# Latent attention: score chunks of 1024 keys in place of 512, and a rule by width for who turns the probabilities

## The chip, the cores and the metric

The kernel runs on one core of one Trainium2 chip. The metric is the device time of one execution in microseconds. Three runs of the kernel before gave 3594.26, 3597.3 and 3606.11 us: the median is 3597.3 us.

## The reference

A trunk of two layers over 2048 tokens of width 1024. Layer 0 mixes tokens with sliding-window attention, layer 1 with multi-head latent attention, and each is followed by a mixture of 32 experts. The change lies in the attention of layer 1 alone. There, for each of 16 heads, with 96 numbers in a query or a key and 64 in a value:

```python
sc = einsum('bqhd,bkhd->bhqk', q, k) * scale
sc = where(kpos <= qpos, sc, -inf)
p = softmax(sc)
o = einsum('bhqk,bkhd->bqhd', p, v)
```

## The kernel before

**Units.** The function `attend` (L1326) works through 256 units. A unit is one head `h` and one block `i` of 128 queries; it sees `i + 1` blocks of 128 keys, so a head has 136 blocks of 128 x 128 probabilities and the whole stage 2176. Within a head the order is 15, 0, 14, 1, ... 8, 7 (the last head runs 0 to 15), so that a large unit and a small one make a pair of 17 blocks, 8 pairs in a head.

**Scores (`scores`, L1380).** A unit's keys are cut into chunks of 512, so a unit has one to four of them, a head 40 and the stage 640. Each chunk takes one PSUM bank from `room()` (L1343), which hands out the seven buffers `sc`. TensorE multiplies high and low halves of queries and keys in three products (L1393 to L1395) and adds the causal mask to the last block (L1397). VectorE takes the maximum of the chunk (L1398); with more than one chunk a second small reduction joins the maxima (L1403). Only then does ScalarE compute the exponentials into a float32 buffer `bpr` (L1407, seven buffers), which frees the bank.

**Turning.** The product with the values needs the probabilities transposed, as a high and a low float16 half. `direct` (L1370) gives about a fifth of the keys to TensorE, by a running debt (`owed[2]`), and in the last head all of the units from 13 on. The others go by a transfer: the high half is copied by VectorE (L1422, two fifths) or ScalarE (L1424), GpSimd subtracts it to make the low half (L1425; VectorE does a sixteenth), the two go into a pack `bpp` of up to 8 blocks (`place`, L1346), and `send` (L1356) has SyncE turn the pack into `bpt` with one transposing transfer (L180). Chunks of different units can share a pack. `turn_unit` (L1429) does TensorE's part two units later: up to four transposes into one bank of `room()` (L1437), ScalarE's copy of the high half (L1441), VectorE's subtraction for the low half (L1442).

**Values (`values`, L1444).** Six units later (`LAG`) TensorE multiplies the turned blocks with the values (L1456, L1457), two instructions a block, and VectorE sums the result of a pair out of PSUM (L1463).

**Order.** In each step of the loop over units the chunks of the new unit's scores alternate with those of the values of the unit six back, then come the turns of the unit two back, and in every second step one entry of `todo`: keys or values of a later head pair (which also take a bank from `room()`), the end of a pair (`finish`, L1471), or output weights. The order in which each engine's queue is written is fixed at build time by a scheduler that follows this program order but moves work that it takes to be ready ahead of work that it takes to be waiting. All transfers of the stage are issued by SyncE, in one queue. The eight PSUM banks are seven `sc` and one `po`.

Of the kernel before, what the change touches and what calls it, by code (L numbers as in the profile page):

```python
# [9 lines left out]
F32 = mybir.dt.float32  # L10
# [110 lines left out]
class Kernel:  # L121
# [1204 lines left out]
    def attend(self, q_d, kr_d, o_d, w_o):  # L1326
        nc, tc = self.nc, self.tc
        V, G, C = nc.vector, nc.gpsimd, nc.scalar
        LAG, PACK, SHARES, TURNED = 6, 8, (2 / 5, 1 / 16), 1 / 5
        with ExitStack() as s:  # L1330
            kp = s.enter_context(tc.tile_pool(name="tb", bufs=1, reuse_waits="tile"))
            wk = s.enter_context(tc.tile_pool(name="tk", bufs=2, reuse_waits="tile"))
# [3 lines left out]
            qb = [self.t(kp, [96, 2, S], F16, f"qb{n}") for n in range(2)]  # L1336
            for n in range(3):
                nc.sync.dma_start(kb[n][NOPE:], kr_d)
            U, heads, todo, owed = {}, {}, [], [0.0, -150.0, 0.0]

            pack = {"n": 0}

            def room():  # L1343
                return self.t(ps, [P, 512], F32, "sc", bufs=7)

            def place(nb):  # L1346
                if pack["n"] + nb > PACK:
# [21 lines left out]

            def direct(h, i, w):  # L1370

                owed[2] += TURNED * w
                if h == B_H - 1 and i >= 13:
                    return True
                if owed[2] > w / 2:
                    owed[2] -= w
                    return True
                return False

            def scores(n, h, i, u, c):  # L1380

                (Qh, Ql), (Kh, Kl) = ([b[h % len(b)][:, x] for x in range(2)] for b in (qb, kb))
                qs = slice(i * P, (i + 1) * P)
                nk = (i + 1) * P
                ncn = -(-nk // 512)
                if c == 0:
                    u["sm"], u["sc"], u["pt"], u["pr"] = self.t(wk, [P, 8], F32, "bsm2", bufs=4), [], [], []
                sm = u["sm"]
                w = min(512, nk - 512 * c)
                ks = slice(512 * c, 512 * c + w)  # L1390
                sc = room()
                last = c == ncn - 1
                nc.tensor.matmul(sc[:, :w], Qh[:, qs], Kh[:, ks], start=True, stop=False)  # L1393
                nc.tensor.matmul(sc[:, :w], Qh[:, qs], Kl[:, ks], start=False, stop=False)  # L1394
                nc.tensor.matmul(sc[:, :w], Ql[:, qs], Kh[:, ks], start=False, stop=not last)  # L1395
                if last:
                    nc.tensor.matmul(sc[:, w - P:w], self.ident_b, self.causal, start=False, stop=True)  # L1397
                V.tensor_reduce(sm[:, c:c + 1], sc[:, :w], axis=AX.X, op=ALU.max, negate=ncn == 1)  # L1398
                u["sc"].append((sc, w))
                if not last:  # L1400
                    return
                if ncn > 1:
                    V.tensor_reduce(sm[:, 4:5], sm[:, 0:ncn], axis=AX.X, op=ALU.max, negate=True)  # L1403
                nm = sm[:, 4:5] if ncn > 1 else sm[:, 0:1]
                for sc, w in u["sc"]:
                    pr = self.t(wk, [P, 512], F32, "bpr", bufs=7)
                    C.activation(pr[:, :w], sc[:, :w], AF.Exp, bias=nm)  # L1407
                    if direct(h, i, w):
                        u["pr"].append((len(u["pt"]), pr, w))
                        u["pt"].append(None)  # L1410
                        continue
                    pp, pt = place(w // P)
                    u["pt"].append(pt)
                    pb = pr[:, :w].rearrange("p (k q) -> p k q", q=P)

                    mine = [False, False]
                    for part, share in enumerate(SHARES):
                        owed[part] += share * w
                        if owed[part] > w / 2 and not (part and mine[0]):
                            mine[part], owed[part] = True, owed[part] - w  # L1420
                    if mine[0]:
                        V.tensor_copy(pp[:, :, 0], pb)  # L1422
                    else:
                        C.activation(pp[:, :, 0], pb, AF.Copy)  # L1424
                    (V if mine[1] else G).tensor_tensor(pp[:, :, 1], pb, pp[:, :, 0], op=ALU.subtract)  # L1425
                if n % 2 and (h == B_H - 1 or n == len(units) - 1):
                    send()

            def turn_unit(u):  # L1429

                many = len(u["pr"]) > 1
                for c, pr, w in u["pr"]:
                    if many and c % 2 == 0:
                        two = self.t(wk, [P, PACK, 2, P], F16, "bpt", bufs=9)
                    tp = room()
                    for k in range(0, w, P):
                        nc.tensor.transpose(tp[:, k:k + P], pr[:, k:k + P], self.ident)  # L1437
                    out = two[:, c % 2 * 4:] if many else self.t(wk, [P, 4, 2, P], F16, "bpd", bufs=5)
                    out = u["pt"][c] = out[:, :w // P]
                    tp = tp[:, :w].rearrange("p (k q) -> p k q", q=P)  # L1440
                    C.activation(out[:, :, 0], tp, AF.Copy)  # L1441
                    V.tensor_tensor(out[:, :, 1], tp, out[:, :, 0], op=ALU.subtract)  # L1442

            def values(h, i, n, u, c):  # L1444

                second = n % 2
                j = units[n ^ 1][1]
                if c == 0 and not second:
                    U["po"] = self.t(ps, [P, 512], F32, "po", bufs=1)
                slot = i > j  # L1450
                po = U["po"][:, slot * 130:(slot + 1) * 130]
                v = self.vbs[h // 2 % 2]
                pt = u["pt"][c]
                for k in range(4 * c, min(4 * c + 4, i + 1)):
                    vv = v[:, k, h % 2]
                    nc.tensor.matmul(po, pt[:, k % 4, 0], vv, start=k == 0, stop=False)  # L1456
                    nc.tensor.matmul(po[:, :HD + 1], pt[:, k % 4, 1], vv[:, :HD + 1], start=False, stop=k == i)  # L1457
                if second and 4 * c + 4 > i:
# [47 lines left out]
            for n in range(len(units) + LAG):  # L1506
                ns = nv = 0
                if n < len(units):
                    h, i = units[n]
                    at = n % NT  # L1510
                    U[n] = {}
                    ns = i // 4 + 1
                    if at == LAG - 2 and h % 2 == 0:
                        deliver(h + 1)
                        if h + 2 < B_H:
                            todo += [lambda q=q, f=nxt[2]: f(q) for q in range(4)]
                        else:
                            todo += [lambda c=c: project_weights(c) for c in range(KC)]
                    if at == 0 and h % 2 and h + 2 < B_H:

                        out = [(kb[(h + 1 + e) % 3], slice(64 * e, 64 * e + 64)) for e in range(2)]
                        todo += [lambda q=q, f=nxt[1], o=out: f(q, o) for q in range(4)]
                    if at == 10 and h % 2 and h + 1 < B_H:
                        deliver(h + 1)
                        if h + 3 < B_H:
                            nxt = self.pair((h + 3) // 2, room)
                            nxt[0]()
                if n >= LAG:
                    hv, iv = units[n - LAG]
                    nv = iv // 4 + 1  # L1530
                for c in range(max(ns, nv)):
                    if c < ns:
                        scores(n, h, i, U[n], c)
                    if c < nv:
                        values(hv, iv, n - LAG, U[n - LAG], c)
                if n - 2 in U and U[n - 2]["pr"]:
                    turn_unit(U[n - 2])
                if n >= LAG:
                    del U[n - LAG]
                if todo and (n % 2 or n >= len(units) - NT):  # L1540
                    todo.pop(0)()
# [113 lines left out]
```

## Time and profile before

| | |
|---|---|
| profiled execution, its own time | 3594.12 us |
| its span, first to last instruction | 3592.2 us |
| mean granted TensorE clock | 0.927 |
| busy over the span: TensorE (PE), VectorE (DVE), ScalarE (ACT), GpSimd (POOL) | 83%, 77%, 59%, 44% |
| latent attention | from about 1704 to 2563 us of the span |

Busy times are unions of an engine's instructions; idle time is put down to the engine or transfer whose signal ended it. Matmuls overlap in the pipeline, so the duration of one in a row is longer than the distance to the next. A transfer's row gives the time in which SyncE's queue issued it; its landing comes later.

### The profile page before, as it was taken

To read this page: it belongs to the slowest core of one execution; us is meant where nothing else is said; L and a number is where in the kernel's file an instruction comes from. 1 tells how busy PE (TensorE), PEld (TensorE's weight loads), DVE (VectorE), ACT (ScalarE), POOL (GpSimd) and SP (SyncE) were. 2 spreads that over 40 slices of the span, in tenths; PEclk is the share of its full clock that TensorE was granted. 3 is DMA by queue.
4 is the path that set the end of the run, shared out by engine and by line. 5 is a ranking of instruction groups with operands and counts; after the bars stand their busy time and mean duration, and the time that the engine had idled before them with its cause. 6 is when DMAs were issued, how large, how long until landed. Compare 5 with 4: busy or idle time off the path is not lost. (4 is left out here: it accounts for less than half of the span.)

```text
span 3592.2 us, 83083 instructions
## 1 busy us (share of the span) xinstructions
PE 2973.6 (83%) x32611; PEld 2239.1 (62%) x32611; DVE 2767.1 (77%) x5272; ACT 2109.6 (59%) x3669; POOL 1576.8 (44%) x1562
## 2 busy tenths in 40 slices
PE   7888878699998886788888889887897799989960
PEld 3444443399988885344566556665443799988860
DVE  5776758788877787776788888788688788877858
ACT  5766622166667675543777777776411566677753
POOL 2544434412323325564566666666244123233245
PEclk9999989899999998899999999999998899999985
DMA  8988779899999998996799999999699899999996
GB/s 225 192 190 174 137 201 311 261 325 350 337 351 359 357 361 290 242 236 179 133 185 179 169 164 182 159 186 190 155 294 281 287 342 351 362 357 362 359 343 242
DMA packets 1112188, 930.56 MB, mean 259 GB/s; under 512 B 933633, under 2 KB 992257, under 8 KB 1060865
## 3 DMA queue, kind: packets, MB, share of 16 engines
q1 hardware_dynamic: 1078112, 817.04, 85.3%
q0 software_dynamic: 33664, 108.03, 8.2%
q8 instruction: 259, 4.24, 0.5%
q14 instruction: 153, 1.25, 0.1%
HBM read 538.32 MB, written 158.60 MB: 194 GB/s over the span
## 5 line engine op out<-in xcount | busy, mean ns | idle before, releaser
L176 DVE SCALAR_TENSOR_TENSOR wl<-raw,wh 128x2048 f16<-128x2048 f32 x322 | 843.2, 2625 | 186.4 <-ACT wh L171 185.6
L908 PE MATMUL pg<-xt,wh 128*128 128x128 f16 (+5 forms) x4096 | 819.9, 230 | 62.4 <-DMA xt<-xs 48.0
L910 PE MATMUL pg<-xt,wl 128*128 128x128 f16 (+5 forms) x4096 | 807.0, 230 | 43.1 <-DVE wl L176 42.9
L909 PE MATMUL pg<-xt,wh 128*128 128x128 f16 (+5 forms) x4096 | 819.2, 230 | 0.0
L171 ACT ACTIVATE wh<-raw 128x2048 f16<-128x2048 f32 x384 | 722.1, 1900 | 92.1 <-DMA raw<-in_moe_w_dram 85.3
L1425 POOL TENSOR_TENSOR bpp<-bpr,bpp 128x512 f16<-128x512 f32 (+3 forms) x448 | 475.8, 1080 | 277.9 <-DVE bpp L1422 179.3
L938 POOL DMA_DIRECT2D y<-yr x256 | 146.3, 573 | 717.9 <-DVE yr L930 541.8
L928 PE MATMUL py<-hh,wl 128*128 128x128 f16 (+5 forms) x2048 | 418.2, 232 | 35.1 <-POOL wl L174 35.1
L910 PEld LDWEIGHTS <-wl 128*128 128x128 f16 x4096 | 403.0, 99 | 54.3 <-DVE wl L176 54.2
L1398 DVE TENSOR_REDUCE bsm<-sc 128x1 f32<-128x512 f32 (+3 forms) x640 | 373.8, 602 | 81.1 <-PE sc L1395 62.8
L908 PEld LDWEIGHTS <-wh 128*128 128x128 f16 x4096 | 405.2, 99 | 47.0 <-issue 30.2
L927 PE MATMUL py<-hl,wh 128*128 128x128 f16 (+5 forms) x2048 | 418.0, 231 | 8.8 <-DVE hl L174 8.8
L926 PE MATMUL py<-hh,wh 128*128 128x128 f16 (+5 forms) x2048 | 417.5, 231 | 1.7 <-ACT wh L171 1.2
L909 PEld LDWEIGHTS <-wh 128*128 128x128 f16 x4096 | 405.5, 99 | 18.8 <-issue 18.8
L1407 ACT ACTIVATE bpr<-sc,bsm 128x512 f32<-128x512 f32 (+3 forms) x640 | 352.5, 630 | 94.1 <-DVE bsm L1403 88.5
L174 POOL TENSOR_TENSOR wl<-raw,wh 128x2048 f16<-128x2048 f32 x62 | 253.3, 4086 | 263.1 <-ACT wh L171 198.9
L1456 PE MATMUL po<-v,bpt 128*128 128x130 f16 x1750 | 208.1, 224 | 87.1 <-DMA bpt<-bpp 78.7
L1393 PE MATMUL sc<-kb,qb 96*128 96x512 f16 (+3 forms) x640 | 232.6, 363 | 26.1 <-ACT bpr L1407 12.0
L928 PEld LDWEIGHTS <-wl 128*128 128x128 f16 x2048 | 203.6, 100 | 49.7 <-POOL wl L174 40.1
L1456 PEld LDWEIGHTS <-bpt 128*128 128x128 f16 x1750 | 161.5, 99 | 116.2 <-DMA bpt<-bpp 98.9
L1394 PE MATMUL sc<-kb,qb 96*128 96x512 f16 (+3 forms) x640 | 230.5, 360 | 0.0
L1395 PE MATMUL sc<-kb,qb 96*128 96x512 f16 (+3 forms) x640 | 229.0, 360 | 0.0
(323 smaller groups left out, 7799.5 us busy)
## 6 DMA issues: line engine op xcount, KB each, us to landing
raw<-in_moe_w_dram SPq DMA_DIRECT2D x384, 1024.0 KB, 8.6
y<-yr POOLq DMA_DIRECT2D x144, 160.0 KB, 7.6
x<-pxr SPq DMA_DIRECT2D x32, 512.0 KB, 4.8
cz<-x SPq DMA_DIRECT2D x32, 512.0 KB, 8.7
xs<-zero SPq DMA_DIRECT2D x32, 384.0 KB, 5.2
q<-qn SPq DMA_DIRECT2D x48, 256.0 KB, 2.7
y<-yr POOLq DMA_DIRECT2D x72, 128.0 KB, 7.2
ax<-in_x_t_dram SPq DMA_DIRECT2D x16, 512.0 KB, 4.1
```

Source lines behind the costliest of these rows:

```text
L171: nc.scalar.activation(hi, src, AF.Copy, scale=scale)
L176: eng.scalar_tensor_tensor(lo, src, scale, hi, op0=ALU.mult, op1=ALU.subtract)
L908: nc.tensor.matmul(out, hi, x[:, c], start=c == 0, stop=False)
L909: nc.tensor.matmul(out, hi, x[:, KC + c], start=False, stop=False)
L910: nc.tensor.matmul(out, lo, x[:, c], start=False, stop=c == KC - 1)
L926: nc.tensor.matmul(out, hi, hh[:, m], start=m == 0, stop=False)
L927: nc.tensor.matmul(out, hi, hl[:, m], start=False, stop=False)
L928: nc.tensor.matmul(out, lo, hh[:, m], start=False, stop=m == F // P - 1)
L1398: V.tensor_reduce(sm[:, c:c + 1], sc[:, :w], axis=AX.X, op=ALU.max, negate=ncn == 1)
L1407: C.activation(pr[:, :w], sc[:, :w], AF.Exp, bias=nm)
L1425: (V if mine[1] else G).tensor_tensor(pp[:, :, 1], pb, pp[:, :, 0], op=ALU.subtract)
L1456: nc.tensor.matmul(po, pt[:, k % 4, 0], vv, start=k == 0, stop=False)
```

## The change

Chunks become 1024 keys wide (`WIDE`), in a PSUM tile of two banks, three such tiles (`sc`), and one single bank (`one`) for everything else that called `room()`. A unit has one or two chunks, a head 24, the stage 384. A chunk is still written by products of at most 512 keys, but there is one maximum, one exponential, one copy and one subtraction for it. `bpr` becomes four buffers of 1024. `direct` gives to TensorE each chunk of 512 keys or fewer (units 0 to 3, and the second chunk of units 8 to 11), in the last head also the units from 13 on. Transposes go through the single bank, 512 keys at a time. In `scores` the step is now named `step`.

```diff
-        LAG, PACK, SHARES, TURNED = 6, 8, (2 / 5, 1 / 16), 1 / 5
+        LAG, PACK, SHARES = 6, 8, (2 / 5, 1 / 16)
...
+            WIDE = PACK * P
+            U, heads, todo, owed = {}, {}, [], [0.0, -150.0]
...
             def room():
-                return self.t(ps, [P, 512], F32, "sc", bufs=7)
+                return self.t(ps, [P, 512], F32, "one", bufs=1)
...
             def direct(h, i, w):
-                owed[2] += TURNED * w
-                if h == B_H - 1 and i >= 13:
-                    return True
-                if owed[2] > w / 2:
-                    owed[2] -= w
-                    return True
-                return False
+                return w <= 512 or h == B_H - 1 and i >= 13
...
-                ncn = -(-nk // 512)
+                ncn = -(-nk // WIDE)
...
-                w = min(512, nk - 512 * c)
-                ks = slice(512 * c, 512 * c + w)
-                sc = room()
+                w = min(WIDE, nk - WIDE * c)
+                sc = self.t(ps, [P, WIDE], F32, "sc", bufs=3)
                 last = c == ncn - 1
-                nc.tensor.matmul(sc[:, :w], Qh[:, qs], Kh[:, ks], start=True, stop=False)
-                nc.tensor.matmul(sc[:, :w], Qh[:, qs], Kl[:, ks], start=False, stop=False)
-                nc.tensor.matmul(sc[:, :w], Ql[:, qs], Kh[:, ks], start=False, stop=not last)
-                if last:
-                    nc.tensor.matmul(sc[:, w - P:w], self.ident_b, self.causal, start=False, stop=True)
+                for at in range(0, w, 512):
+                    n = min(512, w - at)
+                    ks, out = slice(WIDE * c + at, WIDE * c + at + n), sc[:, at:at + n]
+                    end = last and at + n == w
+                    nc.tensor.matmul(out, Qh[:, qs], Kh[:, ks], start=True, stop=False)
+                    nc.tensor.matmul(out, Qh[:, qs], Kl[:, ks], start=False, stop=False)
+                    nc.tensor.matmul(out, Ql[:, qs], Kh[:, ks], start=False, stop=not end)
+                    if end:
+                        nc.tensor.matmul(sc[:, w - P:w], self.ident_b, self.causal, start=False, stop=True)
...
-                    pr = self.t(wk, [P, 512], F32, "bpr", bufs=7)
+                    pr = self.t(wk, [P, WIDE], F32, "bpr", bufs=4)
...
             def turn_unit(u):
-                many = len(u["pr"]) > 1
                 for c, pr, w in u["pr"]:
-                    if many and c % 2 == 0:
-                        two = self.t(wk, [P, PACK, 2, P], F16, "bpt", bufs=9)
-                    tp = room()
-                    for k in range(0, w, P):
-                        nc.tensor.transpose(tp[:, k:k + P], pr[:, k:k + P], self.ident)
-                    out = two[:, c % 2 * 4:] if many else self.t(wk, [P, 4, 2, P], F16, "bpd", bufs=5)
+                    if w <= 512:
+                        out = self.t(wk, [P, 4, 2, P], F16, "bpd", bufs=4)
+                    else:
+                        out = self.t(wk, [P, PACK, 2, P], F16, "bpt", bufs=9)
                     out = u["pt"][c] = out[:, :w // P]
-                    tp = tp[:, :w].rearrange("p (k q) -> p k q", q=P)
-                    C.activation(out[:, :, 0], tp, AF.Copy)
-                    V.tensor_tensor(out[:, :, 1], tp, out[:, :, 0], op=ALU.subtract)
+                    for at in range(0, w, 512):
+                        tp, n = room(), min(512, w - at)
+                        for k in range(0, n, P):
+                            nc.tensor.transpose(tp[:, k:k + P], pr[:, at + k:at + k + P], self.ident)
+                        tp, to = tp[:, :n].rearrange("p (k q) -> p k q", q=P), out[:, at // P:(at + n) // P]
+                        C.activation(to[:, :, 0], tp, AF.Copy)
+                        V.tensor_tensor(to[:, :, 1], tp, to[:, :, 0], op=ALU.subtract)
...
-                for k in range(4 * c, min(4 * c + 4, i + 1)):
+                for k in range(PACK * c, min(PACK * c + PACK, i + 1)):
...
-                    ns = i // 4 + 1
+                    ns = i // PACK + 1
...
-                    nv = iv // 4 + 1
+                    nv = iv // PACK + 1
```

## Rows read from the trace of the kernel before

**Rows 1.** Busy time (us) of two stretches: PE, PEld, DVE, ACT, POOL, then clock, DMA share, GB/s.
```profile
1720.00:2540.00 820.00, 712.09 (x7532) 486.47 (x7529) 671.63 (x1478) 598.67 (x1180) 531.56 (x522) 0.95 0.97 173
1993.50:1998.50 5.00, 4.60 (x53) 2.90 (x51) 4.41 (x12) 3.70 (x8) 2.00 (x3) 1.00 1.11 212
```

**Rows 2.** Transfers of 1720 to 2540, all queues.
```profile
DMA packets 477741, 141.47 MB, mean 173 GB/s; under 512 B 466189, under 2 KB 474381, under 8 KB 476301
```

**Rows 3.** Who waited for whom, 1720 to 2540: us in total, times, longest.
```profile
POOL bpp L1425 <- DVE bpp L1422: 174.0, 101, 10.8
...
ACT bpr L1407 <- DVE bsm L1403: 80.9, 79, 3.7
PE po L1456 <- DMA bpt<-bpp: 75.2, 52, 4.9
...
PE sc L1393 <- ACT bpr L1407: 10.0, 15, 1.4
```

**Rows 4.** Groups by line and shape, 1720 to 2540, VectorE: count, busy us, mean ns, idle before.
```profile
L1398 DVE TENSOR_REDUCE bsm<-sc 128x1 f32<-128x512 f32 x430 | 288.9, 682 | 71.7 <-PE sc L1395 62.4 <-PE po L1457 4.0 <-PE sc L1397 3.6
...
L1422 DVE CAST bpp<-bpr 128x512 f16<-128x512 f32 x139 | 79.2, 570 | 13.2 <-ACT bpr L1407 12.9
...
L1398 DVE TENSOR_REDUCE bsm<-sc 128x1 f32<-128x128 f32 x63 | 17.6, 279 | 1.1 <-PE sc L1397 1.0
...
L1403 DVE TENSOR_REDUCE bsm<-bsm 128x1 f32<-128x2 f32 x64 | 9.2, 144 | 0.2
```

**Rows 5.** The same view, ScalarE: exponentials.
```profile
L1407 ACT ACTIVATE bpr<-sc,bsm 128x512 f32<-128x512 f32 x430 | 271.5, 691 | 83.7 <-DVE bsm L1403 80.9 <-POOL bpp L1425 1.3 <-issue 0.3
...
L1407 ACT ACTIVATE bpr<-sc,bsm 128x128 f32<-128x128 f32 x63 | 24.0, 381 | 0.0
```

**Rows 6.** The tile `bpr`: copies of the high half, ns (min/median/max), first and last start.
```profile
L1424 ACT ACTIVATE bpp<-bpr x283: 302/637/741, 1712.3 to 2539.7; 128x512 f16<-128x512 f32 x107, 128x256 f16<-128x256 f32 x16, 128x384 f16<-128x384 f32 x13, 128x128 f16<-128x128 f32 x6
L1422 DVE CAST bpp<-bpr x201: 216/427/1410, 1711.0 to 2541.9; 128x512 f16<-128x512 f32 x67, 128x256 f16<-128x256 f32 x14, 128x384 f16<-128x384 f32 x11, 128x128 f16<-128x128 f32 x9
```

**Rows 7.** Groups by line and shape, GpSimd: subtractions for the low half.
```profile
L1425 POOL TENSOR_TENSOR bpp<-bpr,bpp 128x512 f16<-128x512 f32 x338 | 394.9, 1182 | 241.0 <-DVE bpp L1422 147.6 <-ACT bpp L1424 36.0 <-DVE rs L1478 22.5
...
L1425 POOL TENSOR_TENSOR bpp<-bpr,bpp 128x128 f16<-128x128 f32 x24 | 11.3, 471 | 7.3 <-DVE bpp L1422 7.1 <-DVE bsm L1403 0.2
```

**Rows 8.** TensorE's turns, all of line L1437: duration in ns (min/median/max), first and last start.
```profile
L1437 PE MATMUL sc<-ident,bpr x471: 272/273/456, 1712.2 to 2558.8; 128*128 128x128 f32 x157
```

**Rows 9.** Groups by line and shape again: VectorE's and ScalarE's part of a turn.
```profile
L1442 DVE TENSOR_TENSOR bpd<-sc,bpd 128x512 f16<-128x512 f32 x75 | 51.0, 680 | 2.3 <-ACT bpd L1441 1.6
...
L1441 ACT ACTIVATE bpd<-sc 128x512 f16<-128x512 f32 x75 | 45.2, 602 | 61.6 <-PE sc L1437 59.1 <-PE po L1457 2.0
```

**Rows 10.** Timeline of the stage's end (start us, us): the last turns.
```profile
2551.45 1.04 PE L1437 MATMUL sc<-ident,bpr 128*128 128x128 f32 x8
...
2558.85 3.54 DVE L1442 TENSOR_TENSOR bpt<-sc,bpt 128x512 f16<-128x512 f32 x6
```

**Rows 11.** The tile `bpt`: its transfers' issue in ns (min/median/max), and their landing.
```profile
L180 SPq DMA_TRANSPOSE bpt<-bpp x240: 1255/2020/5223, 1714.5 to 2547.4; - x120
...
DMA to landing us min/median/max: 3.4/4.6/8.6
```

**Rows 12.** Timeline at 1900 us (start us, us): distances between products.
```profile
1900.38 0.38 PE L1393 MATMUL sc<-kb,qb 96*128 96x512 f16 x1
...
1900.60 0.38 PE L1394 MATMUL sc<-kb,qb 96*128 96x512 f16 x1
...
1901.42 0.22 PE L1456 MATMUL po<-v,bpt 128*128 128x130 f16 x1
...
1901.50 0.22 PE L1456 MATMUL po<-v,bpt 128*128 128x130 f16 x1
```

**Rows 13.** Groups by line and shape: the causal mask, one instruction a unit, 1720 to 2540.
```profile
L1397 PE MATMUL sc<-causal,identb 128*128 128x128 bf16 x248 | 55.8, 225 | 0.0
```

More of the change, by code (lines that the diff above doesn't have):

```diff
@@ L1338, in attend @@
                 nc.sync.dma_start(kb[n][NOPE:], kr_d)
-            U, heads, todo, owed = {}, {}, [], [0.0, -150.0, 0.0]
+            WIDE = PACK * P
+            U, heads, todo, owed = {}, {}, [], [0.0, -150.0]
             pack = {"n": 0}
             def room():
-                return self.t(ps, [P, 512], F32, "sc", bufs=7)
+                return self.t(ps, [P, 512], F32, "one", bufs=1)
             def place(nb):
@@ L1370, in direct, with scores @@
             def direct(h, i, w):
-                owed[2] += TURNED * w
-                if h == B_H - 1 and i >= 13:
-                    return True
-                if owed[2] > w / 2:
-                    owed[2] -= w
-                    return True
-                return False
-            def scores(n, h, i, u, c):
+                return w <= 512 or h == B_H - 1 and i >= 13
+            def scores(step, h, i, u, c):
                 (Qh, Ql), (Kh, Kl) = ([b[h % len(b)][:, x] for x in range(2)] for b in (qb, kb))
@@ L1425, in scores @@
                     (V if mine[1] else G).tensor_tensor(pp[:, :, 1], pb, pp[:, :, 0], op=ALU.subtract)
-                if n % 2 and (h == B_H - 1 or n == len(units) - 1):
+                if step % 2 and (h == B_H - 1 or step == len(units) - 1):
                     send()
             def turn_unit(u):
-                many = len(u["pr"]) > 1
                 for c, pr, w in u["pr"]:
-                    if many and c % 2 == 0:
-                        two = self.t(wk, [P, PACK, 2, P], F16, "bpt", bufs=9)
-                    tp = room()
-                    for k in range(0, w, P):
-                        nc.tensor.transpose(tp[:, k:k + P], pr[:, k:k + P], self.ident)
-                    out = two[:, c % 2 * 4:] if many else self.t(wk, [P, 4, 2, P], F16, "bpd", bufs=5)
-                    out = u["pt"][c] = out[:, :w // P]
-                    tp = tp[:, :w].rearrange("p (k q) -> p k q", q=P)
-                    C.activation(out[:, :, 0], tp, AF.Copy)
-                    V.tensor_tensor(out[:, :, 1], tp, out[:, :, 0], op=ALU.subtract)
+                    if w <= 512:
+                        out = self.t(wk, [P, 4, 2, P], F16, "bpd", bufs=4)
+                    else:
+                        out = self.t(wk, [P, PACK, 2, P], F16, "bpt", bufs=9)
+                    out = u["pt"][c] = out[:, :w // P]
+                    for at in range(0, w, 512):
[5 more added lines that the diff above has]
+                        V.tensor_tensor(to[:, :, 1], tp, to[:, :, 0], op=ALU.subtract)
             def values(h, i, n, u, c):
@@ L1453, in values @@
                 pt = u["pt"][c]
-                for k in range(4 * c, min(4 * c + 4, i + 1)):
+                for k in range(PACK * c, min(PACK * c + PACK, i + 1)):
                     vv = v[:, k, h % 2]
-                    nc.tensor.matmul(po, pt[:, k % 4, 0], vv, start=k == 0, stop=False)
-                    nc.tensor.matmul(po[:, :HD + 1], pt[:, k % 4, 1], vv[:, :HD + 1], start=False, stop=k == i)
-                if second and 4 * c + 4 > i:
+                    nc.tensor.matmul(po, pt[:, k % PACK, 0], vv, start=k == 0, stop=False)
+                    nc.tensor.matmul(po[:, :HD + 1], pt[:, k % PACK, 1], vv[:, :HD + 1], start=False, stop=k == i)
+                if second and PACK * c + PACK > i:
                     if n % NT == 1:
```

## The prediction

> **What bounds the kernel now.** The change touches one stage, so I first took the busy times of that stretch alone. In its 820 us TensorE is busy for 712, VectorE for 672, ScalarE for 599, GpSimd for 532, and the transfer engines' share is 0.97 [rows 1]. That share overstates the load: in five microseconds in which only transposes ran it read 1.11, at 212 GB/s [rows 1]; the stage moved 141.5 MB [rows 2], which at that rate is 667 us, 81% of the stretch. So no engine is full. TensorE (87%), VectorE (82%) and the transfers (81%) lie close together, and what TensorE lacks is 108 us. The waits come next: 75 us of those 108 TensorE waited at the value product L1456 for a turned pack, and only 10 us for a free score bank [rows 3]. Behind the packs GpSimd waited 174 us for VectorE's copies, and ScalarE 81 us for the joined maximum [rows 3]. The reader is to see a loop: scores, maximum, exponential, copy, subtraction, transfer, values six units later, with VectorE's queue the busiest link on it. Work taken from VectorE and ScalarE shortens the loop; work added to the transfers lengthens it.
>
> **The change, part by part.**
>
> *Maxima.* A reduction of 512 keys takes 682 ns, of 128 keys 279 [rows 4]: 134 ns for 128 keys and 145 fixed. 640 become 384: 256 x 0.145 = 37 us less. The joining reduction at 144 ns [rows 4] is needed by 8 units of a head, not 12: 64 fewer, 9 us.
>
> *Exponentials and copies.* 691 and 381 ns [rows 5] make 103 for 128 keys and 278 fixed: 256 x 0.278 = 71 us less on ScalarE. Chunks that go by transfer fall from 484, 283 copied by ScalarE and 201 by VectorE [rows 6], to 250 (16 in each of 15 heads, 10 in the last), some 150 and 100. If a copy's least time is 128 keys and its median 512 [rows 6], ScalarE's 302 and 637 ns have 190 fixed and VectorE's 216 and 427 have 146: 25 and 15 us less, and 7 and 3 back for the blocks added below, net 18 and 12. GpSimd's subtractions (1182 and 471 ns [rows 7]: 237 for 128 keys and 234 fixed) fall by 214: 50 us less, and 100 blocks more, 24: net 26.
>
> *Turns on TensorE.* Before there were 471 blocks [rows 8]. After, a head has 20 (units 0 to 3 and 8 to 11 each give 1+2+3+4) and the last head 45 more: 365. Each turned chunk costs VectorE and ScalarE 0.68 and 0.60 us a 512 [rows 9], so 106 blocks fewer save VectorE 16 and ScalarE 14. On TensorE eight in a row took 1.04 us [rows 10]: 106 x 0.13 = **14 us less**, on the engine that is nearest to full; I count it whole.
>
> Together VectorE loses 37+9+12+16 = 74 us of 672, ScalarE 71+18+14 = 103 of 599, GpSimd 26 of 532.
>
> *Transfers.* The same 106 blocks now go by transfer: 1705 become 1811, each 64 KB (two halves of 128 x 128 float16), 6.9 MB or 33 us at 212 GB/s; the transfers' load goes from 81% to 85%. Issues go from 240 [rows 11] to 250; an issue holds SyncE for 2.0 us at the median, half the stretch, so the 20 us more hide in SyncE's idle time. A landing takes 4.6 us at the median against 3.4 at the least [rows 11], so transfers mostly don't queue today.
>
> *The wait at the values.* It is 75 us. Bounds: all of it goes (-75), or the 33 us of transfers come on top (+33). VectorE falls to 73% and ScalarE to 60%, which is where the packs are late; the transfers' own time stays and grows. A wide chunk is also one long chain (exponential 1.1, copy 0.7 to 1.1, subtraction 2.1 us by the slopes above) in place of two short overlapping ones, but it shares its pack with no other unit. I take **-30 us**, a little under half way to the favourable end.
>
> *Score banks.* Seven banks become three pairs, and one chunk of any width takes a pair. A large unit holds two pairs, the small one beside it the third, so the next large unit's first product waits until the first exponential of this one is done. For the pair of units 15 and 0: products 1.3 us twice (six at 0.22 [rows 12]), 8 blocks of values between them at 0.085 [rows 12], 0.7; then a reduction of 1024 keys 1.22, the join 0.14, an exponential 1.10: 5.8, and with four hand-offs of about 0.1 (an estimate) 6.1 us. For 14, 13 and 12 it is 5.8, 5.5 and 5.2, for smaller units less than TensorE's own work. Today a pair takes 820 / 124 = 6.6 us (248 masks are 124 pairs [rows 13]). So with no queueing on VectorE and ScalarE it costs nothing (0); with two queued wide operations of about 0.85 us each, 1.7 us, the four heavy pairs take 7.8, 7.5, 7.2 and 6.9, on average 0.75 too long, 64 x 0.75 = +48. VectorE has 27% free, so I take **+10**.
>
> *The single bank.* Transposes, keys and values of later heads take turns in one bank. A turn of 512 keys holds it for 0.52 + 0.60 + 0.68 and three hand-offs, 2.1 us. In the stage one comes every 6.6 us and its result is wanted four units later, so what collides is covered by scores that are ready; I take 0, and if the cover is gone, four collisions in each of eight head pairs cost up to 2 us each, 64. At the end nothing covers: units 13, 14 and 15 of the last head are 12 turns of up to 512 keys. Before, they lay between 2551.45 and 2562.39 us [rows 10], 10.9 us, at VectorE's pace over several banks. One bank makes them 12 x 2.1 = 25 us: +14, or +5 if unit 13's start earlier, beside the last scores. I take **+11**.
>
> **Sum.** -14 - 30 + 10 + 11 = -23 us on the profiled execution's 3594.1 us (its span 3592.2 and 1.9 around it): 3571. The median of the runs lies 3.2 above that execution, so I forecast 3574.
>
> *A rule against it.* VectorE's copies took 216 to 1410 ns with a median of 427 [rows 6], and the mean at 512 keys is 570 [rows 4], so some waited 0.14 us on average and a few about 1. The Trainium skill (SBUF — State Buffer, Who interferes with whom) says why: such a copy and a GpSimd operation take the same pair of ports as an exclusive lock for a whole instruction. By that rule a wide copy can stand behind a subtraction of 2.1 us.
>
> **The rivals.**
>
> *Score banks decide (slower), 0.22.* The mechanism above with 1.7 us of queueing: +48 +11 - 14 = +45, 3642, if the value wait gives nothing; with half of my 30 back, 3627. It decides once queueing on the way from the last product to the first exponential passes 0.5 us in the heaviest pair. For it: ScalarE starts on the joined maximum with no delay today, but VectorE takes a chunk's maximum at once only where nothing stands in its queue. Against it: today's 10 us of bank waits, and a scheduler that can put value products first.
>
> *Wide copies lock with GpSimd (slower), 0.06.* If each of 100 wide copies waits half a subtraction, 1.07 us, VectorE gets 107 us where the waits cost 201 x 0.14 = 28 before: +79 eats the 74 that it saves. The value wait then stays and the 33 us of transfers are added: -14 + 33 + 10 + 11 = +40, 3637. Against it: GpSimd mostly waits for the copy, not the copy for GpSimd.
>
> *Transfers are the bound (no change), 0.17.* The 33 us eat the gain at the values: -14 + 10 + 11 = +7 at 0 there, 3604; 3590 with half of the 30. For it: 75 of TensorE's idle 108 us end with a landing.
>
> *The wait goes altogether (much faster), 0.10.* -14 - 75 + 11 = -78, 3519.
>
> *The wide instructions don't save their fixed part,* because a pass over two banks costs it twice: 0.03; then the queues stay as they are, and it is the case of no change.
>
> **How the numbers follow.** The forecast has 0.42, spread from 3540 to 3590. 0.3%, 10.8 us, is about what a measurement of this kernel can tell from no change: below 3586.5 is faster, above 3608.1 slower. Faster: nearly all of the forecast's 0.42 and the 0.10, 0.52. Same: 0.17 + 0.03, less a little, 0.19. Slower: 0.28 with a trace of the transfer case, 0.29. The range of 8 in 10 must reach into both sides: from 3520, where all the waits go, to 3638, which holds most of the slower cases. The forecast's own range is 3540 to 3590.
>
> **What would show it.** Right: 384 maxima at up to 1.22 us and 384 exponentials at up to 1.10; VectorE's busy time in the stage down by some 70 us, ScalarE's by 100; 365 transposes; the wait of L1456 for `bpt` well below 75 us; the last 12 turns spaced by about 2 us. Wrong: the first score product waiting for exponentials by far more than 10 us (score banks), wide copies near 1.7 us on average (lock), or landings above 4.6 us with the value wait at 75 or more (transfers).

## The result, and the profile after

The change made the kernel **slower**: 3725.8 us at the median of four runs (3722.6 to 4434.1; the longest ran at a granted clock of 0.66 where the others had 0.92, and the ratio leaves it out) against 3595.8 before (3588.8 to 3606.1 in four), a ratio of 1.0356, interval 1.0323 to 1.0389. That is some 128 us more, where 23 fewer were forecast, and it lies above the whole range. The profiled execution took 3727.6 us, its span 3725.8.

The time came in the attention stage. Two stretches of the kernel after, in the columns of [rows 1]: the same 820 us as there, and the whole stage, first product to last turn.

```profile
1720.00:2540.00 820.00, 658.13 (x6655) 440.72 (x6653) 531.81 (x910) 481.14 (x682) 457.18 (x279) 0.93 0.88 158
1704.00:2693.00 989.00, 782.22 (x7729) 523.11 (x7727) 644.62 (x1090) 570.81 (x812) 526.87 (x321) 0.91 0.85 154
```

And the whole stage of the kernel before:

```profile
1704.00:2563.00 859.00, 743.92 (x7834) 508.44 (x7832) 701.34 (x1539) 622.96 (x1225) 544.76 (x535) 0.95 0.95 170
```

The stage grew from 859 to 989 us, 130 of the 133 us between the two profiled executions. Every engine is busy for a smaller share of it, and the transfers too: nothing became full. TensorE is idle for 207 us of it instead of 115, 92 more; the other 38 are busy time, though it has fewer instructions, at a granted clock that averages 0.91 where it was 0.95 (a mean of stretches at the two levels, 1.2 and 2.4 GHz).

Who waits for whom, in the waits of 1720 to 2640 (columns as in [rows 3]; the stretch is longer than there, and leaves out the last turns as that one did):

```profile
POOL bpp L1424 <- DVE bpp L1421: 212.7, 77, 9.1
...
ACT bpr L1406 <- DVE bsm L1402: 119.5, 81, 5.0
...
PE po L1456 <- DMA bpt<-bpp: 85.4, 65, 4.4
...
PE sc L1392 <- ACT bpr L1406: 46.2, 40, 6.6
...
PE one L1439 <- DVE kb L176: 10.9, 10, 2.1
...
PE one L196 <- DVE bpd L1442: 7.7, 13, 1.0
```

Over the whole kernel the page puts 55 us of the idle time ahead of the score products on the exponentials, in the groups by line:

```profile
L1392 PE MATMUL sc<-kb,qb 96*128 96x512 f16 (+3 forms) x640 | 235.9, 369 | 62.8 <-ACT bpr L1406 55.1
```

The value wait didn't fall, it stands at 85 us where it was 75 [rows 3]. The first score product now waits for an exponential, that is, for a score tile to come free: 46 us against 10. The turns, and the keys and values of later heads, wait for one another in `one`. And the last 12 turns, which stood at VectorE's pace [rows 10], are spaced by 2.5 us, in the instructions on the tile `bpt`, first of the kernel before, then after (ns min/median/max, first and last start):

```profile
L1442 DVE TENSOR_TENSOR bpt<-sc,bpt x12: 424/681/692, 2553.3 to 2561.7; 128x512 f16<-128x512 f32 x10, 128x256 f16<-128x256 f32 x1, 128x384 f16<-128x384 f32 x1
```
```profile
L1442 DVE TENSOR_TENSOR bpt<-one,bpt x12: 424/692/692, 2663.6 to 2691.4; 128x512 f16<-128x512 f32 x10, 128x256 f16<-128x256 f32 x1, 128x384 f16<-128x384 f32 x1
```

First start to last end, 9.1 us became 28.4.

### The profile page after: what moved, and what is told of

Its sections match the earlier page's. It is cut to its first block, busy times and chain, and to the rows that moved or that the text cites. A ratio compares the mean times of both kernels' runs of the same rounds, so it can differ in the third digit from the quotient of the medians.

```text
span 3725.8 us, 81551 instructions
## 1 busy us (share of the span) xinstructions
PE 3006.0 (81%) x32505; PEld 2244.8 (60%) x32505; DVE 2709.2 (73%) x4823; ACT 2056.3 (55%) x3256; POOL 1555.1 (42%) x1348
## 5 line engine op out<-in xcount | busy, mean ns | idle before, releaser
L1424 POOL TENSOR_TENSOR bpp<-bpr,bpp 128x1024 f16<-128x1024 f32 (+3 forms) x234 | 455.6, 1960 | 390.0 <-DVE bpp L1421 221.9
L1397 DVE TENSOR_REDUCE bsm<-sc 128x1 f32<-128x1024 f32 (+7 forms) x384 | 340.2, 906 | 111.3 <-PE sc L1394 82.5
L1406 ACT ACTIVATE bpr<-sc,bsm 128x1024 f32<-128x1024 f32 (+7 forms) x384 | 312.9, 864 | 137.1 <-DVE bsm L1402 128.5
L1456 PE MATMUL po<-v,bpt 128*128 128x130 f16 x1856 | 218.0, 230 | 106.1 <-DMA bpt<-bpp 85.7
L1392 PE MATMUL sc<-kb,qb 96*128 96x512 f16 (+3 forms) x640 | 235.9, 369 | 62.8 <-ACT bpr L1406 55.1
L1456 PEld LDWEIGHTS <-bpt 128*128 128x128 f16 x1856 | 179.1, 103 | 121.6 <-DMA bpt<-bpp 109.5
L1393 PE MATMUL sc<-kb,qb 96*128 96x512 f16 (+3 forms) x640 | 236.7, 370 | 0.0
L1394 PE MATMUL sc<-kb,qb 96*128 96x512 f16 (+3 forms) x640 | 234.2, 369 | 0.0
```

Source lines behind the costliest of these rows:

```text
L1456: nc.tensor.matmul(po, pt[:, k % PACK, 0], vv, start=k == 0, stop=False)
```

## The experiments

Two theories stood against each other at first: that the score tiles decide (three pairs that come free late, where seven single banks did), and that the transfers or the packs do (wide copies and subtractions, fewer and larger buffers). A third asked what the single bank costs alone. The change can be taken apart into steps, so the runs form a ladder from either end. Each ratio is to the kernel before, run beside it.

**The rule alone.** Only `direct` is changed, so that TensorE turns what it turns after the change.

```diff
-                owed[2] += TURNED * w
-                if h == B_H - 1 and i >= 13:
-                    return True
-                if owed[2] > w / 2:
-                    owed[2] -= w
-                    return True
-                return False
+                return h == B_H - 1 and i >= 13 or i < 4 or 8 <= i < 12 and len(u_pt) == 2
```

> The kernel before, with only the rule for who turns as in the changed kernel: TensorE turns units 0 to 3, the last 512-or-fewer keys of units 8 to 11, and the last head's units from 13 on; chunks of 512 keys and seven single score banks stay. 365 turned blocks in place of 471, 33 us more of transfers. Transfers theory: most of the 130 us comes here, 60 us or more over the kernel before (3655 us and up). Score-bank, single-bank and wide-instruction theories: between 15 us less and 30 us more (3580 to 3625).

Measured: 1.0014 (0.9994 to 1.0034), no difference that can be told. Had the 14 us that fewer turns were to save on TensorE and the 33 us of added transfers both counted in full, it would have been 19 us more, above the interval of -2 to 12 us. How much of either counted isn't shown.

**One bank for the rest, six for scores.** The kernel before, with the scores kept narrow.

```diff
             def room():
-                return self.t(ps, [P, 512], F32, "sc", bufs=7)
+                return self.t(ps, [P, 512], F32, "one", bufs=1)
...
-                sc = room()
+                sc = self.t(ps, [P, 512], F32, "sc", bufs=6)
```

> The kernel before with its seven score banks split into six for scores and a single one for turns, keys, values and the last transposes, as in the changed kernel; chunks of 512 and the old rule stay. Single-bank theory: 60 us or more over the kernel before (3655 and up), of which 14 to 18 in the last twelve turns. Score-bank theory (it is the pairs that hurt): 15 to 35 us, mostly the last turns (3610 to 3630). Transfers and wide-instruction theories: the same 15 to 35.

Measured: 1.0111 (1.0075 to 1.0146), 40 us. Its waits of 1720 to 2548 and its last turns:

```profile
PE po L1456 <- DMA bpt<-bpp: 31.5, 25, 3.2
...
PE sc L1393 <- ACT bpr L1407: 21.2, 36, 2.3
...
PE po L1456 <- ACT bpd L1441: 18.7, 24, 3.3
...
PE one L1437 <- DVE kb L176: 8.9, 9, 2.0
...
PE one L1437 <- DVE bpd L1442: 7.4, 13, 1.8
```
```profile
L1442 DVE TENSOR_TENSOR bpt<-one,bpt x12: 425/691/692, 2570.3 to 2600.1; 128x512 f16<-128x512 f32 x10, 128x256 f16<-128x256 f32 x1, 128x384 f16<-128x384 f32 x1
```

The last 12 turns take 30.4 us, 21 more than before: half of the 40. The other half lies in the stage, where a head's turns, keys and values collide in the one bank, the values wait for turned chunks (19 us at `bpd`), and scores, with one bank fewer to draw on, wait 21 us for an exponential where it was 10 [rows 3]. The wait for transfers fell at the same time, from 75 us [rows 3] to 32, so how these add up to 19 us isn't shown.

**Two narrow chunks in one pair,** without and with the rule: the first attempt at taking the pairs alone.

```diff
-                sc = self.t(ps, [P, 512], F32, "sc", bufs=6)
+                if c % 2 == 0:
+                    u["two"] = self.t(ps, [P, 1024], F32, "sc", bufs=3)
+                sc = u["two"][:, c % 2 * 512:c % 2 * 512 + 512]
```

> As e2_one_bank, but two chunks of 512 share a pair of banks, three pairs in all, and a lone chunk takes a whole pair; every instruction still works on 512 keys. Score-bank theory: 60 to 100 us over e2_one_bank, near the changed kernel (3690 to 3730), with waits of the first score product for exponentials of 50 us or more where they were 10. Single-bank theory: within 20 us of e2_one_bank. Wide-instruction theory: within 30 us of e2_one_bank, the loss comes only with the wide instructions.

> As e3_pairs, with the changed kernel's rule for who turns as well: what is left between this one and the changed kernel is the width of the instructions (and the probability buffers, seven of 512 against four of 1024). Wide-instruction theory: 60 us or more under the changed kernel (3665 or less). Score-bank theory: within 30 us of it on either side, since wide instructions only save their fixed parts (3695 to 3755). Transfers theory: 40 us or more over e3_pairs.

Measured: 1.0728 (1.0689 to 1.0766) and 1.0687 (1.0650 to 1.0724). These two don't isolate what they were made for. (The diff is against the run with six score banks.) The products of a pair's second half here wait until the maximum of its first half has been read, which neither kernel has to do: the waits of the first of the two, 1720 to 2784, show products held by maxima.

```profile
PE sc L1395 <- ACT bpr L1409: 21.3, 25, 3.4
...
PE sc L1395 <- DVE bsm L1400: 14.7, 20, 2.8
```

They overstate the pairs by an unknown amount, so the next step was built from the other end.

**From the kernel after: narrow maxima and exponentials in the same pairs.** All products of a pair come first, then the instructions of 512.

```diff
-                V.tensor_reduce(sm[:, c:c + 1], sc[:, :w], axis=AX.X, op=ALU.max, negate=ncn == 1)
+                for at, out in enumerate(parts):
+                    V.tensor_reduce(sm[:, 2 * c + at:2 * c + at + 1], out, axis=AX.X, op=ALU.max, negate=nk <= 512)
...
-                    C.activation(pr[:, :w], sc[:, :w], AF.Exp, bias=nm)
+                    for at, part in zip(range(0, w, 512), sc):
+                        C.activation(pr[:, at:min(at + 512, w)], part, AF.Exp, bias=nm)
```

> The changed kernel with maxima and exponentials of 512 keys again, both halves of a pair multiplied before the first of its maxima; pairs of banks, wide copies and subtractions, single bank and rule stay. What it adds is the fixed parts only. Score-bank theory: a pair is held some 0.4 to 0.6 us longer, so 20 to 70 us over the changed kernel (3745 to 3795). Theory that the wide instructions themselves make the loss, because everything behind one on its engine waits longer: 40 us or more under the changed kernel (3685 or less).

**The same with six single score banks in place of the three pairs,** the maximum of each right after its products.

```diff
-                pair = self.t(ps, [P, WIDE], F32, "sc", bufs=3)
...
-                    ks, out = slice(WIDE * c + at, WIDE * c + at + n), pair[:, at:at + n]
+                    ks, out = slice(WIDE * c + at, WIDE * c + at + n), self.t(ps, [P, 512], F32, "sc", bufs=6)[:, :n]
```

> As e6_narrow_in_pairs, but each 512 keys of scores in a bank of their own, six single banks in place of three pairs; wide copies and subtractions, four wide probability buffers, the single bank for turns and the rule stay. Score-bank theory: back to the cost of single bank and rule alone, some 25 to 55 us over the kernel before (3625 to 3655), that is 70 to 100 under the changed kernel. Theory of wide copies, subtractions and few probability buffers: it stays within 30 us of the changed kernel (3695 and up).

**And with seven banks that everything shares,** as before the change: `room()` gives a `"sc"` of seven again, for scores too.

```diff
-                return self.t(ps, [P, 512], F32, "one", bufs=1)
+                return self.t(ps, [P, 512], F32, "sc", bufs=7)
```

> As e7_single_banks, with turns, keys and values taking their banks from the same seven as the scores, as in the kernel before: against that one only the rule, the wide copies and subtractions and their buffers are new. Score-bank and single-bank theories: within 20 us of the kernel before (3580 to 3620), the last turns back at 11 us. Theory of wide copies and subtractions: 40 us or more over the kernel before.

Measured: 1.0463 (1.0418 to 1.0507), 1.0197 (1.0154 to 1.0241), 1.0066 (1.0042 to 1.0091). Narrow instructions in pairs are *slower* than the wide ones, by 39 us; the same instructions in single banks are 96 us faster than in pairs, though they use the same six banks; sharing all seven takes off 47 more. The 96 us hold two things that no run separates: three tiles that come free together with both their banks, and a first maximum that starts only after the products of both halves, which a shared pair brings with it. What TensorE's score products waited for, first in the pairs (1720 to 2684), then in the six single banks (1720 to 2570):

```profile
PE po L1459 <- DMA bpt<-bpp: 75.0, 61, 4.2
PE sc L1392 <- ACT bpr L1409: 51.6, 45, 8.4
PE one L1442 <- DVE bsm L1404: 26.3, 17, 3.7
```
```profile
PE po L1457 <- DMA bpt<-bpp: 66.2, 52, 4.6
...
PE sc L1391 <- ACT bpr L1407: 17.0, 37, 1.6
```

And the two stages, first product to last turn, in the columns of [rows 1], in the same order:

```profile
1700.00:2736.00 1036.00, 810.43 (x7725) 529.67 (x7723) 674.33 (x1412) 610.58 (x1069) 528.66 (x321) 0.89 0.80 148
```
```profile
1696.00:2626.00 930.00, 778.25 (x7726) 518.65 (x7723) 680.45 (x1412) 610.52 (x1069) 526.56 (x321) 0.91 0.93 165
```

Of the 106 us between these two stages, TensorE's direct wait for an exponential makes 35. Another 32 us are busy time on the same products, at a granted clock of 0.89 against 0.91. The rest is in other waits, that of the turns first (L1442 above).

**Two pairs and three single banks,** chunks of 512 or fewer keys in the singles, with the turns.

```diff
-                return self.t(ps, [P, 512], F32, "one", bufs=1)
+                return self.t(ps, [P, 512], F32, "one", bufs=3)
...
-                sc = self.t(ps, [P, WIDE], F32, "sc", bufs=3)
+                sc = self.t(ps, [P, WIDE], F32, "sc", bufs=2) if w > 512 else room()
```

> The changed kernel with two pairs of banks for chunks over 512 keys and three single banks for chunks of up to 512 and for turns, keys and values. Pairs wanted per pair of banks: 16 of a head's chunks on two, where it was 24 on three, so as many; what a small unit held of a pair is freed, and the single bank becomes three. Score-bank theory, with small units' long holds as the cost: 20 to 60 us under the changed kernel (3665 to 3705). Single-bank theory: 30 to 50 under it. If only the large units' own chain counts: within 20 us of it, on either side.

Measured: 1.0309 (1.0263 to 1.0356), 17 us below the kernel after by the point values, the intervals overlapping. The last 12 turns now take 15.7 us, 13 fewer, which is most of it:

```profile
L1442 DVE TENSOR_TENSOR bpt<-one,bpt x12: 415/679/693, 2653.5 to 2668.5; 128x512 f16<-128x512 f32 x10, 128x256 f16<-128x256 f32 x1, 128x384 f16<-128x384 f32 x1
```

In the stage itself, taking the small chunks out of the pairs gained next to nothing. Its waits of 1720 to 2640 show a score wait some 10 us shorter (46 in the kernel after) and a value wait 41 us longer (85 there):

```profile
PE po L1456 <- DMA bpt<-bpp: 126.7, 84, 7.1
...
PE sc L1392 <- ACT bpr L1406: 36.5, 40, 6.0
```

So the small chunks' hold of a pair is not what makes the 96 us; why the value wait grew is not shown.

**More buffers behind the scores:** six wide `bpr` and six packs in place of four and eight, in the kernel after, and in the one with seven banks.

```diff
-                    pr = self.t(wk, [P, WIDE], F32, "bpr", bufs=4)
+                    pr = self.t(wk, [P, WIDE], F32, "bpr", bufs=6)
```

> The changed kernel with six probability buffers of 1024 in place of four, and six packs of halves in place of eight to make room. Score-bank theory: within 15 us of the changed kernel, since what frees a pair is the exponential and that waits for the joined maximum, not for a buffer. Theory that four wide buffers are too few (a turned chunk holds one for two units): 15 to 60 us under it.

> The same exchange of buffers in e8_seven_banks, which lay 0.66% over the kernel before. Too-few-buffers theory: back to the rule alone (e1_rule, 0.14% over), 15 us or more under e8_seven_banks. Theory that the wide copies and subtractions cost it by making a pack wait for 1024 keys of one engine's work: within 8 us of e8_seven_banks.

Measured: 1.0322 (1.0290 to 1.0354) and 1.0075 (1.0043 to 1.0107), against 1.0356 and 1.0066 without. The first lies 12 us under the kernel after, the intervals overlapping, the second 3 us over its counterpart. So more buffers for the exponentials, at the price of two packs, bring nothing that can be told; what six of them with all eight packs would do was not tried.

**Narrow copies and subtractions,** in the kernel with seven banks, packs and buffers as after the change.

```diff
+                    for at in range(0, w, 512):
+                        n = min(512, w - at)
+                        part = slice(at // P, (at + n) // P)
...
-                        V.tensor_copy(pp[:, :, 0], pb)
+                            V.tensor_copy(pp[:, part, 0], pb[:, part])
...
-                    (V if mine[1] else G).tensor_tensor(pp[:, :, 1], pb, pp[:, :, 0], op=ALU.subtract)
+                        (V if mine[1] else G).tensor_tensor(pp[:, part, 1], pb[:, part], pp[:, part, 0], op=ALU.subtract)
```

> e8_seven_banks with copies and subtractions of 512 keys again; packs stay one chunk each, probability buffers four of 1024. e8_seven_banks lay 0.66% over the kernel before, e1_rule 0.14%. Theory that wide copies and subtractions cost it (a subtraction of 2.1 us starts only when the whole copy is done): back to 0.0 to 0.3% over the kernel before. Theory that it is the packs, which no longer mix units: 0.5 to 0.9% over.

Measured: 1.0014 (0.9995 to 1.0032). With the rule kept, packs of one chunk and four wide `bpr`, but everything done 512 keys at a time in seven shared banks, the kernel is back at the time of the one before. What TensorE waited for without and then with narrow copies, 1720 to 2560 in both:

```profile
PE po L1457 <- DMA bpt<-bpp: 95.9, 71, 4.2
...
PE sc L1391 <- DVE bpd L1443: 13.7, 11, 2.9
```
```profile
PE po L1460 <- DMA bpt<-bpp: 89.9, 70, 3.6
...
PE sc L1391 <- DVE bpd L1446: 3.4, 4, 1.5
```

The values' wait for a transfer differs by 6 us. The scores' wait for a bank that a turn still holds, because VectorE has not yet subtracted its low half, differs by 10.

**Fewer copies on VectorE,** in the kernel before: the share of keys that VectorE copies, from 2/5 to 1/5 and to none.

```diff
-        LAG, PACK, SHARES, TURNED = 6, 8, (2 / 5, 1 / 16), 1 / 5
+        LAG, PACK, SHARES, TURNED = 6, 8, (1 / 5, 1 / 16), 1 / 5
```

> The kernel before with one fifth of the copies of the high half on VectorE in place of two fifths: VectorE loses some 100 copies or 50 us, ScalarE gains some 60. It tests the step that work taken from VectorE brings the packs in time. If so: the value product's wait falls by 20 us or more and the time by 10 to 40 (3560 to 3590). If VectorE's load is not what makes the packs late: within 10 us of the kernel before. If ScalarE's exponentials come later for it and hold the score banks: 10 to 40 us over it.

> The kernel before with no copy of the high half on VectorE at all (e11_share had half of them, and was 0.79% faster). VectorE loses another 50 us, ScalarE gains some 65 and becomes as full as TensorE. If VectorE's load is what counts: 10 to 25 us under e11_share (3555 to 3575). If the gain of e11_share came from an even load: 0 to 30 us over it, as exponentials wait behind copies.

Measured: 0.9921 (0.9896 to 0.9946) and 0.9923 (0.9900 to 0.9947), 3581.8 and 3577.0 us: some 28 us under the kernel before, so **faster than both kernels**, and the second half of the copies brought nothing more. The waits of the first, 1720 to 2540:

```profile
POOL bpp L1425 <- DVE bpp L1422: 114.2, 53, 9.9
PE po L1456 <- DMA bpt<-bpp: 78.6, 55, 4.5
POOL bpp L1425 <- ACT bpp L1424: 75.7, 48, 7.2
ACT bpr L1407 <- DVE bsm L1403: 38.7, 49, 2.4
```

VectorE's queue got shorter as meant (ScalarE's wait for the joined maximum fell from 81 us [rows 3] to 39), but the value wait did not, 79 us against 75. From the first score product to the start of the last turn's subtraction this execution took 845 us against 860 before, and the one with no share 851. By which wait the gain comes isn't shown.

## Why the prediction was wrong

As a ladder from before to after, the ratios times 3600 us give:

| step | us |
|---|---|
| the rule (fewer turns, more transfers) | +5 (interval -2 to +12) |
| packs of one chunk, four wide `bpr` | 0 |
| wide copies and subtractions | +19 |
| one bank for turns, keys and values, six for scores | +47 (+40 alone) |
| three pairs for six single banks, maxima after both halves | +96 |
| wide maxima and exponentials | -39 |
| sum | +128 |

Each step is the difference of two ratios whose intervals reach some 0.2 to 0.45% to either side, so each is good to some 10 to 22 us; that the pairs are the largest is not in doubt.

**The step that failed is "Score banks".** It was taken at +10, with bounds of 0 and +48. Measured are +96 for the pairs, and +57 net of what the wide maxima and exponentials give back. Two things were wrong in it. First, the chain from a unit's first product to the end of its first exponential was put at 6.1 us with nothing queueing. Worked out instruction by instruction from the trace after, as means over units 15 of heads 1 to 13: 2.75 us to the end of the last product (3.3 forecast), 1.96 to the end of its maximum (1.3), 1.46 to the start of the exponential (0.4), 1.11 for the exponential: 7.28. The products went faster than forecast, and still the rest was 1.7 us longer. That is the queueing of 1.7 us that the step had named as its bad end and set aside because VectorE would have 27% free. It had 35% free over the stage (645 us busy of 989). **A share of free time says nothing about the queue in front of one instruction.** Here is ScalarE's timeline (start us, us) at the small unit 0, one block of 128 keys:

```profile
2009.30 2.12 ACT L1406 ACTIVATE bpr<-sc,bsm 128x1024 f32<-128x1024 f32 x2
2011.31 1.05 ACT L1423 ACTIVATE bpp<-bpr 128x1024 f16<-128x1024 f32 x1
2012.26 0.28 ACT L1441 ACTIVATE bpd<-one 128x128 f16<-128x128 f32 x1
2012.41 0.38 ACT L1406 ACTIVATE bpr<-sc,bsm 128x128 f32<-128x128 f32 x1
```

And VectorE's, where the third of the three maxima is that unit's:

```profile
2006.60 2.55 DVE L1397 TENSOR_REDUCE bsm<-sc 128x1 f32<-128x1024 f32 x3
2009.07 0.14 DVE L1402 TENSOR_REDUCE bsm<-bsm 128x1 f32<-128x2 f32 x1
```

Its maximum is there at 2009.15 us, its exponential of 0.4 us starts at 2012.41, behind two wide exponentials, a wide copy and a turn. Over the heads, unit 0 keeps two banks for 5.94 us, of which it waits 3.96; units 1 to 7 keep theirs 4.3 to 6.6.

Second, the step priced the four heavy pairs of units alone and put the others at nothing, as shorter than TensorE's own work. Worked out product by product from the trace after, the first score products waited 55 us for an exponential (12 before, over the whole kernel), each time for that of the chunk three back, which had held the same pair. 40 of the 55 stand before the first chunk of a large unit in the heads 0 to 14, and these wait for the first chunk of the large unit before it, which is the path that the step had named. But only 20 of them are waits for units 15 to 12; the other 20 are for units 11 to 8, which the step let go free. Only 10 stand before a small unit's chunk in these heads, though the small units make 44 of the 143 us for which a head holds pairs; the other 5 are in the last head.

Counted over the stretch 1760 to 2500 us, from each tile's first product to the end of its last exponential, all three pairs were held for 56% of the time. All seven banks before, with the turns, keys and values that shared them (to VectorE's last read), were held for 23%, and by score chunks alone for 1%. A TensorE that can't start the next scores then has nothing to do but values, which wait for transfers, and the granted clock of the stage fell from 0.95 to 0.91. That the rest of the 96 us, beyond the direct waits, follows from these is argued, not shown.

**"The single bank" (+11) was mis-sized.** The collisions in the stage were put at 0, with 64 if their cover were gone; the run with that edit alone leaves 40 - 21 = 19 for them. The end was put at +14 or +5, from 12 turns of 2.1 us; they take 2.5 apart, +19 to +21. The whole is +40 to +47.

**"The wait at the values" (-30) did not come.** It is 85 us after, inside its bounds of -75 and +33 but at the wrong side of zero. The wide copies and subtractions, priced as a saving of their fixed parts, cost 19 us of time. A pack now starts its transfer only behind one long subtraction:

```profile
L1424 POOL TENSOR_TENSOR bpp<-bpr,bpp 128x1024 f16<-128x1024 f32 x147 | 312.1, 2129 | 251.1 <-DVE bpp L1421 101.8 <-ACT bpp L1423 65.0 <-issue 38.2
```

GpSimd's row in the groups by shape of 1720 to 2640, count, busy us, mean ns, idle before. It stood idle behind the copies for longer than before. That this longer chain makes the 19 us is not shown: between the executions with wide and with narrow copies the value wait differed by only 6 us, and the wait for banks that turns held, behind VectorE's queue, by 10.

**What was right.** The counts and the durations of single instructions came out. In the same view:

```profile
L1397 DVE TENSOR_REDUCE bsm<-sc 128x1 f32<-128x1024 f32 x151 | 184.0, 1220 | 83.8 <-PE sc L1394 81.0 <-PE sc L1396 0.8 <-PE po L1457 0.7
...
L1406 ACT ACTIVATE bpr<-sc,bsm 128x1024 f32<-128x1024 f32 x150 | 166.0, 1112 | 125.6 <-DVE bsm L1402 119.5 <-PE po L1457 3.4 <-POOL bpp L1424 2.1
```

1220 and 1112 ns, forecast 1.22 and 1.10 us; a pass over two banks pays its fixed part once (1220 is two of 682 [rows 4] less 144), so that rival fell. The work saved over the whole stage was less than the durations promised: VectorE 701 to 645 us, 57 of 74; ScalarE 623 to 571, 52 of 103. (In these sums the turns were taken at 16 and 14 us, where 106 blocks at 0.68 and 0.60 us for four are 18 and 16.) Instructions that follow one another overlap, so a mean duration counts a part of the fixed time twice. Three maxima of 512 in a row, in VectorE's timeline of the kernel before:

```profile
1984.70 1.96 DVE L1398 TENSOR_REDUCE bsm<-sc 128x1 f32<-128x512 f32 x3
```

1.96 us, not 3 x 0.682 = 2.05: by this row each that follows another overlaps it by 0.04. Over the 74 pairs of such maxima that follow each other without a gap in that trace the median is 0.08. So a maximum less saves some 0.07 to 0.10 and not 0.145, and the 37 us become 17 to 27. On ScalarE it is more. Two wide exponentials in a row took 2.12 us in the timeline above, 0.10 less than two of 1.112, so an exponential less saves 0.18 and not 0.278, and the 71 us become 46. The Trainium skill (ScalarE: Activation LUTs, What ACT_TABLE_LOAD costs) gives about 93 ns for this overlap of consecutive activations, and the trace agrees with its 0.10 us. These two account for 10 to 20 us where VectorE's saving fell 17 short, and for 25 of ScalarE's 51; where the rest stayed is open.

**The rivals.** "Score banks decide" had the right mechanism and the right sign at 0.22, and its 3627 to 3642 stays 84 us below the result: it carried the +48 bound, which left out the lighter pairs of units, the +11 for the single bank, and no price for the wide copies. "Transfers are the bound" fell with the rule alone: 106 blocks more changed nothing that could be told. Its other sign, landings above 4.6 us, can't be read, since only the trace before gives landing times. "Wide copies lock with GpSimd" asked for wide copies near 1.7 us:

```profile
L1421 DVE CAST bpp<-bpr 128x1024 f16<-128x1024 f32 x41 | 30.6, 745 | 23.5 <-ACT bpr L1406 18.8 <-issue 3.9 <-DMA qb<-q 0.7
```

745 ns on average. The rule that stood beside that rival (the Trainium skill, SBUF — State Buffer, Who interferes with whom), by which such a copy can be shut out for a whole GpSimd instruction, would let a few be long. The longest here took 1861 ns, and no run separates such cases from the 19 us of the wide copies and subtractions.

## What to carry to other kernels

Price a buffer by how long it is held, by every pair of users that follow each other on it and not only the longest: from the producer's first write to the consumer's last read, with what stands in the consumer's queue, times the number of uses, against the number of buffers that come free independently. Merging buffers to make instructions wide halves that number, and here it cost 96 us to save 39. Look also at who waits for whom: a user can hold a buffer long and still make few others wait, as the small units did here. And an engine with a quarter of its time free can still be late at the one instruction that frees the buffer, so take the bad end of such an estimate unless a timeline shows the queue empty there.

## What was not expected of the hardware

An instruction over two adjacent banks is worth something in itself: 39 us of the kernel's time, good to some 20, come from 384 maxima and exponentials in place of 640, and a maximum over 1024 keys took 1220 ns where two of 512 average 1364. What remains open is a layout that keeps it without the pairs' price; two pairs with three single banks got 17 us back, and an order in which the small unit's exponential goes ahead of the large one's copies was not tried. Neither was the smaller copy share of 1/5 or none combined with any part of the change.
